# The second MLP layer's column halves run two row blocks apart, and its outputs leave one per chunk

## The chip, the cores and the metric

The kernel runs on one core of a Trainium2 chip. The metric is the device time of one execution in microseconds; a kernel's time is the median of its runs. TensorE (PE in the profile) multiplies, VectorE (DVE) and ScalarE (ACT) work on tiles in SBUF and PSUM, SyncE (SP) issues the loads and the last stores, GpSimd (POOL) issues the other transfers. Each engine runs its instructions in an order that is fixed when the program is built, and waits on semaphores where an operand is not there yet.

## The reference, cut to what matters

One layer on 512 tokens of 2048 features, in float32:

```python
hn = rms_norm(x, norm_mix)
x = x + neighbourhood_attention(hn, w_qkv, q_gain, k_gain, rel_bias, w_o)
h = rms_norm(x, norm_mlp)
a = relu(h @ w1)          # w1: 2048 x 8192
x = x + (a * a) @ w2      # w2: 8192 x 2048
```

The change touches the last line alone: a product of 512 x 8192 by 8192 x 2048, added to the residual.

## The kernel before

The program has four stages: the projections and the attention, the output projection (whose residual sum goes to `y_sum` in DRAM), the first layer of the MLP (from 778.1 us of the span), and the second (from 1419.6 us to the end).

**Units and chunks.** Both MLP layers are cut into `Pair` units. A unit multiplies all 512 tokens by a weight block of 2048 rows and 1024 columns: four blocks of 512 rows (b = 0 to 3), each seen as a 2 x 2 matrix of quarters, multiplied by seven products instead of eight. `Pair.chunks()` lists the 28 pairs (m, b): first m = 1, 5, 6, 4 for each block in turn (FIRST, chunks 0 to 15), then m = 2, 3, 7 for each block (SECOND, chunks 16 to 27). A chunk is one 128 x 1024 weight tile of 512 KB and twelve 128 x 512 matmuls on it (L248). The first layer has eight units, h0 to h7; the second has eight, yc_p, where c (0 to 3) is the four blocks of rows and p (0, 1) the half of the 2048 output columns; they run y0_0, y0_1, y1_0 and so on to y3_1.

**What a chunk needs.** SP loads the weight tile (L193) some six chunks ahead. For m = 5, 6, 4 and 7 DVE adds the tile before it (L217). ACT makes the high part `wh` (L233), DVE the rest `wl` (L235), both about three chunks ahead of the matmuls. DVE does its instructions in program order, so a tile that isn't there holds all that stands behind it. Raw tiles rotate through ten buffers (`raw`), high and low parts through three (`hl`): a load is issued only when the `wl` that read the buffer's old tile is done.

**Left operands.** h units leave squared activations; `left_window` turns them by 32 transposes per unit in eight windows and writes seven left operands for each block of rows to `z_t` in DRAM (POOL: L710, L711, L721). A y unit needs 28 of them, each 256 KB as read, for its four blocks. `pass_on` loads them (L759, on SP) one after each chunk of the unit before and splits them 1.5 chunks later (a step, `STEP`, is a quarter of a chunk's work; ACT L554, DVE L556). The two units of one c use the same operands, so h7, y0_1, y1_1 and y2_1 carry 28 such loads, and y0_0, y1_0, y2_0, y3_0 and y3_1 none.

**Outputs.** The products end in PSUM banks named x, y, z and w in the trace. At the end of a unit `evict` makes eight tiles of 256 KB: two `c` behind m = 2 of the last block, two `u` behind m = 3, and `t`, `p`, `t`, `p` behind m = 7. `take_out` sends each at once as an accumulating DMA on POOL's queue (L748) to `y_sum`, 48 in all; the units of c = 3 add `y_sum`, loaded ahead by `prefetch`, and store to the output on SP's queue (L746).

**What sets the order.** `run` emits chunk by chunk; `u.after` is called behind each chunk's matmuls; `later(lag, fn)` puts a step off by so many positions. From that the framework's scheduler makes each engine's order: it keeps roughly to the order of emission, but lets an instruction go ahead that it takes to be ready. So loads and adds (L217) may stand up to nine chunks ahead of their matmuls on SP and DVE, further than the six and three chunks that `run` gives them.

Of the kernel before, what the change touches and what calls it, by code (L numbers as in the profile page):

```python
# [14 lines left out]
ALU = mybir.AluOpType  # L15
AX = mybir.AxisListType

P = 128
T = 512
D = 2048  # L20
# [5 lines left out]
NCH = HID // D  # L26
# [6 lines left out]
NB = KT // 4  # L33
# [8 lines left out]
STEP, WAIT, PAIR = 1, 5, 3  # L42


class Unit:
# [7 lines left out]
    def __init__(self, name, src, act, done, kind):  # L53
        self.name, self.src, self.act, self.done, self.kind = name, src, act, done, kind
        self.n = KT // 4 if kind == "narrow" else KT
        self.raw, self.parts, self.ps = {}, {}, None
        self.load, self.before, self.after, self.lag = None, None, None, 0


class Pair:  # L60
# [16 lines left out]
    QUARTER = {1: (0, 0), 5: (0, 1), 6: (1, 1), 4: (1, 0), 2: (1, 0), 3: (1, 1), 7: (0, 1)}  # L77
    CHAIN = {5: 1, 6: 5, 4: 6, 7: 3}

    def __init__(self, name, w, row, col, comb, take):  # L80
        self.name, self.w, self.row, self.col, self.comb, self.take = name, w, row, col, comb, take
        self.raw, self.parts, self.banks, self.after = {}, {}, {}, None
        self.t, self.u, self.p4, self.p5 = {}, {}, {}, {}

    def chunks(self):
        return [(self, (m, b)) for stage in (self.FIRST, self.SECOND) for b in range(NB) for m in stage]

    def quarter(self, m, b):
        r, c = self.QUARTER[m]
        r, c = self.row + (4 * b + 2 * r) * P, self.col + c * T  # L90
        return self.w[r // (2 * P), c // T]


# [1 line left out]
def natten_mlp_kernel(ctx, tc, x_t, gains, w_qk, w_v, bias, w_o, w1, w2, out_t):  # L95
    nc = tc.nc
# [8 lines left out]
    def wtile(name, dt=F32):  # L105
        return tiles.tile([P, T], dt, tag="w", name=name)

    def bank(name):
        return psum.tile([P, T], F32, tag="b", name=name)
# [8 lines left out]
    def kept(ins):  # L118
        return tc.keep_in_program_order(ins) if pos[0] < pinned else ins

    def pair(name):
        return wtile(f"{name}h", F32R), wtile(f"{name}l", F32R)
# [49 lines left out]
    def later(lag, fn):  # L172
        side.append((pos[0] + lag, fn))

    def start(steps):

        wait = next(steps, None)
        if wait is not None:
            later(wait, lambda: start(steps))

    def run_side(until):
        while True:
            due = sorted((s for s in side if s[0] <= until), key=lambda s: s[0])
            if not due:
                return
            for s in due:
                side.remove(s)
                s[1]()
# [20 lines left out]
    def split_raw(u, i, first):  # L209
# [22 lines left out]
        else:  # L232
            kept(nc.scalar.activation(h, s, AF.Copy))  # L233
            yield 2 * STEP
            kept(nc.vector.tensor_tensor(out=l, in0=s, in1=h.bitcast(F32), op=ALU.subtract))  # L235

    def multiply_pair(u, i):
        m, b = i
        x = u.BANK[m]
        if x not in u.banks:  # L240
            u.banks[x] = [bank(f"{x}_{u.name}_{j}") for j in range(2)]
        wh, wl = u.parts.pop(i)
        ah, al = u.comb[b][m]
        for k in range(2):
            for j in range(2):
                c = slice(k * HALF + j * P, k * HALF + (j + 1) * P)
                for n, (a, w) in enumerate(((ah, wh), (ah, wl), (al, wh))):
                    nc.tensor.matmul(out=u.banks[x][j], lhsT=a[:, c], rhs=w[:, k],  # L248
                                     start=(m in u.FIRST and b + k + n == 0), stop=(b == NB - 1 and k == 1 and n == 2),
                                     skip_group_check=True)  # L250
                pos[0] += 1
                if 2 * k + j < 3:
                    run_side(pos[0])
        if b == NB - 1:
            start(evict(u, m))
        if u.after is not None:
            u.after(m, b)
        run_side(pos[0])
# [153 lines left out]
    class Head:  # L412
        def __init__(self, h):
            self.h = h
            self.p = {}
# [105 lines left out]
    for g in range(NG):  # L521
        u = Unit(f"v{g}", lambda i, g=g: w_v[i // 2, g], xa, v_done(g), "tokens")
# [24 lines left out]
    xc = [{} for _ in range(NB)]  # L547
    sq_a = wtile("sq_a")

    def parts_of(dst, m, src, name):  # L550

        h, l = pair(name)
        view = lambda z: z.rearrange("p (k n) -> p k n", k=2)
        nc.scalar.activation(view(h), src, AF.Copy)  # L554
        yield STEP
        nc.vector.tensor_tensor(out=view(l), in0=src, in1=view(h).bitcast(F32), op=ALU.subtract)  # L556
        dst[m] = (h, l)
        yield STEP
# [28 lines left out]
    y_sum = {(c, n): dram.tile([P, T], F32, name=f"y_{c}_{n}", tag=f"y_{c}_{n}") for c in range(QB) for n in range(NG)}  # L587
# [16 lines left out]
    def window():  # L604
        if windows:
            windows.pop(0)()
# [49 lines left out]
    for g in range(NG):  # L656
        u = Unit(f"o{g}", lambda i, g=g: w_o[i // 2, g], oa, o_done(g), "wide")
# [6 lines left out]
    FP = HID // (2 * T)  # L664

    z_t = [dram.tile([P, 7, 2, HALF], F32, name=f"z_{i}", tag=f"z_{i}") for i in range(2 * FP)]
# [8 lines left out]
    def take_hidden(p):  # L675
        zs = {}

        def take(c, half, src, add, minus=False):
            if add is None:
                t = wtile(f"z_{p}_{c}_{half}")  # L680
            else:
                t = join(src, add, minus)
                src = t
            nc.scalar.activation(t, src, AF.Relu, scale=r_a[:, c:c + 1])
            zs[c, half] = t
            if len(zs) == 8:
                for n in range(8):
                    windows.append(left_window(p, n // 4, n // 2 % 2, n % 2, zs))
        return take
# [35 lines left out]
    def take_out(p, last):  # L725
        ys = {}

        def prefetch():
            for c in range(QB):
                for half in range(2):  # L730
                    ys[c, half] = wtile(f"ys_{p}_{c}_{half}")
                    nc.sync.dma_start(out=ys[c, half], in_=y_sum[c, 2 * p + half])

        def take(c, half, src, add, minus=False):
            rows, cols = slice(c * P, (c + 1) * P), slice((2 * p + half) * T, (2 * p + half + 1) * T)
            if add is not None:
                if last:
                    nc.vector.tensor_tensor(out=add, in0=add, in1=ys[c, half], op=ALU.add)
                t = join(src, add, minus)
            elif last:  # L740
                t = join(src, ys[c, half], False)
            else:
                t = wtile(f"c_{p}_{c}_{half}")
                nc.scalar.activation(t, src, AF.Copy)
            if last:
                nc.sync.dma_start(out=out_t[rows, cols], in_=t)  # L746
            else:
                nc.gpsimd.dma_start(out=y_sum[c, 2 * p + half], in_=t, accum_op=ALU.add)  # L748
        return take, prefetch

    def pass_on(dst, block):


        order = (2, 4, 1, 5, 6, 3, 7)
        loaded = {}

        def load(m, b):
            t = loaded[m, b] = wtile(f"zr{m}_z{block}_{b}")
            nc.sync.dma_start(out=t.rearrange("p (k n) -> p k n", k=2), in_=z_t[4 * block + b][:, order.index(m)])  # L759

        def split_left(m, b):
            yield from parts_of(dst[b], m, loaded.pop((m, b)).rearrange("p (k n) -> p k n", k=2), f"a{m}_z{block}_{b}")

        def after(m, b):
            load(m, b)
            later(6 * STEP, lambda: start(split_left(m, b)))
        return after

    pairs, comb = [], xc
    for p in range(FP):  # L770
        u = Pair(f"h{p}", w1, 0, 2 * p * T, comb, take_hidden(p))
        pairs.append(u)
    zc = [[{} for _ in range(NB)] for _ in range(NCH)]
    for c in range(NCH):
        for p in range(2):
            take, prefetch = take_out(p, c == NCH - 1)
            u = Pair(f"y{c}_{p}", w2, c * D, 2 * p * T, zc[c], take)
            u.prefetch = prefetch if c == NCH - 1 else None
            pairs.append(u)
    for n, u in enumerate(pairs):  # L780
        hand = None
        if n >= FP - 1 and (n - FP + 1) % 2 == 0 and n < len(pairs) - 1:
            block = (n - FP + 1) // 2
            hand = pass_on(zc[block], block)

        def after(m, b, n=n, u=u, hand=hand):
            if m in u.SECOND:
                if n == 0 and m == 2 and b == 0:
                    start(norm_a())
                window()  # L790
            if m == 4 and b == NB - 1 and n >= FP and u.prefetch is not None:
                u.prefetch()
            if hand is not None:
                hand(m, b)
        u.after = after
        chunks += u.chunks()

# [53 lines left out]
```

## Time and profile before

| | us |
|---|---|
| median of three runs | 2081.96 (2080.67 to 2084.63) |
| the profiled execution | 2081.29 |
| its span, first to last instruction | 2079.5 |
| second MLP layer, in that span | 1419.6 to 2073.5 |

Engines, busy share of the span: PE 98%, weight loads 81%, DVE 74%, ACT 50%, POOL 6%. The mean granted clock of TensorE is 0.995 of its full level.

With PE busy nearly all the time there are two things to look for in a stretch: how long it takes beside another with the same matmuls, and whether PE is idle in it or busy for longer at a lower clock. A table by stretches shows both: its length, PE's busy time, the granted clock and the busy share of the DMA engines. A timeline of one engine shows how long it sat idle ahead of an instruction and what released it; a list by one source line gives the time from a DMA's issue to its landing.

### The profile page before, as it was taken

How to read it: one execution, taken by the hardware profiler on the slowest of the kernel's cores; microseconds unless marked ns; L12 is line 12 of the kernel's file. 1: busy time of each engine (PE TensorE's matmuls, PEld its weight loads, DVE VectorE, ACT ScalarE, POOL GpSimd, SP SyncE). 2: the span in 40 equal slices, each digit the busy share in tenths (PEclk: the TensorE clock that was granted, in tenths of full speed). 3: DMA queues.
4: the chain of work that ended last, by engine and by line, in shares of the span. 5: the costliest groups of instructions: out<-in, count | busy, mean ns of one | idle time of the engine just before them, and what ended most of it. 6: DMA issues, size and time to landing. Idle time of an engine off the chain costs nothing. (4 is left out here: it accounts for less than half of the span.)

```text
span 2079.5 us, 25226 instructions
## 1 busy us (share of the span) xinstructions
PE 2044.1 (98%) x9330; PEld 1684.3 (81%) x9330; DVE 1546.5 (74%) x1884; ACT 1045.5 (50%) x1412; POOL 116.7 (6%) x166
## 2 busy tenths in 40 slices
PE   9999999999999999999999999999989999999998
PEld 7888888888888888888888888887877877778787
DVE  6674674774774469778878878798879778779786
ACT  6663563653663445544545545565445445346333
POOL 0000000000000000010110110100201011010000
PEclk9999999999999999999999999999999999999999
DMA  7222222222233346565866757778689598688874
GB/s 289 101 92 83 100 92 92 96 90 96 99 101 127 112 137 211 193 217 199 274 202 226 269 180 255 270 255 304 226 295 286 187 272 279 204 261 278 256 243 147
DMA packets 127900, 400.15 MB, mean 192 GB/s; under 512 B 15008, under 2 KB 15008, under 8 KB 127776
## 3 DMA queue, kind: packets, MB, share of 16 engines
q1 hardware_dynamic: 110736, 352.37, 50.3%
q0 software_dynamic: 16896, 46.15, 7.8%
q8 instruction: 73, 1.20, 0.2%
q14 instruction: 51, 0.42, 0.1%
q10 hardware_dynamic: 144, 0.02, 0.0%
HBM read 348.14 MB, written 50.33 MB: 192 GB/s over the span
## 5 line engine op out<-in xcount | busy, mean ns | idle before, releaser
L233 ACT ACTIVATE wh_h<-w_h 128x1024 fp32r<-128x1024 f32 x224 | 237.6, 1060 | 275.0 <-PE y_h L248 83.7
L233 ACT ACTIVATE wh_y<-w_y 128x1024 fp32r<-128x1024 f32 x224 | 236.5, 1059 | 234.2 <-PE y_y L248 69.0
L235 DVE TENSOR_TENSOR wl_h<-w_h,wh_h 128x1024 fp32r<-128x1024 f32 x224 | 272.8, 1221 | 77.4 <-ACT wh_h L233 76.7
L235 DVE TENSOR_TENSOR wl_y<-w_y,wh_y 128x1024 fp32r<-128x1024 f32 x224 | 271.0, 1219 | 24.5 <-ACT wh_y L233 24.0
L217 DVE TENSOR_TENSOR w_y<-w_y,w_y 128x1024 f32<-128x1024 f32 x128 | 156.1, 1220 | 70.9 <-DMA w_y<-in_w 68.1
L217 DVE TENSOR_TENSOR w_h<-w_h,w_h 128x1024 f32<-128x1024 f32 x128 | 155.1, 1219 | 42.9 <-DMA w_h<-in_w 42.8
L235 DVE TENSOR_TENSOR wl_o<-w_o,wh_o 128x1024 fp32r<-128x1024 f32 x32 | 39.1, 1223 | 58.7 <-ACT wh_o L233 58.6
L233 ACT ACTIVATE wh_o<-w_o 128x1024 fp32r<-128x1024 f32 x32 | 33.9, 1059 | 80.0 <-PE mm_o L302 66.2
L233 ACT ACTIVATE wh_q<-w_q 128x1024 fp32r<-128x1024 f32 x32 | 34.0, 1062 | 77.8 <-PE mm_q L302 30.2
L235 DVE TENSOR_TENSOR wl_q<-w_q,wh_q 128x1024 fp32r<-128x1024 f32 x32 | 39.2, 1225 | 43.6 <-ACT wh_q L233 42.3
L235 DVE TENSOR_TENSOR wl_k<-w_k,wh_k 128x1024 fp32r<-128x1024 f32 x32 | 39.1, 1222 | 37.9 <-ACT wh_k L233 37.9
L233 ACT ACTIVATE wh_k<-w_k 128x1024 fp32r<-128x1024 f32 x32 | 34.0, 1062 | 50.8 <-PE mm_q L302 31.1
L233 ACT ACTIVATE wh_v<-w_v 128x1024 fp32r<-128x1024 f32 x31 | 32.8, 1058 | 47.4 <-PE mm_v L302 23.4
L235 DVE TENSOR_TENSOR wl_v<-w_v,wh_v 128x1024 fp32r<-128x1024 f32 x31 | 37.9, 1223 | 23.0 <-ACT wh_v L233 22.6
L600 POOL DMA_DIRECT2D y<-x1t_0s x4 | 2.3, 583 | 770.1 <-ACT x1t_0s L599 770.1
L711 POOL DMA_DIRECT2D z<-zt x32 | 17.7, 553 | 453.0 <-ACT zt L706 452.9
L554 ACT ACTIVATE a_z_0h<-zr_z 128x512 fp32r<-128x512 f32 x28 | 17.6, 627 | 50.4 <-DMA zr_z<-z 48.5
L509 ACT ACTIVATE t<-t,st 128x256 f32<-128x256 f32 x64 | 32.0, 501 | 10.6 <-DVE st L505 10.6
L706 ACT ACTIVATE zt<-zt 128x512 f32<-128x512 f32 x64 | 37.1, 580 | 0.0
L248 PE MATMUL y_y<-wl_y,a_z_1h 128*128 128x512 f32 x64 | 26.6, 416 | 8.4 <-DVE wl_y L235 8.4
L248 PE MATMUL z_y<-wl_y,a_z_0h 128*128 128x512 f32 x64 | 26.7, 418 | 6.8 <-DVE wl_y L235 6.8
L554 ACT ACTIVATE a_z_3h<-zr_z 128x512 fp32r<-128x512 f32 x28 | 17.5, 626 | 29.6 <-DMA zr_z<-z 29.6
(1435 smaller groups left out, 6304.2 us busy)
## 6 DMA issues: line engine op xcount, KB each, us to landing
w_h<-in_w SPq DMA_DIRECT2D x224, 512.0 KB, 4.3
w_y<-in_w SPq DMA_DIRECT2D x224, 512.0 KB, 4.6
zr_z<-z SPq DMA_DIRECT2D x112, 256.0 KB, 5.3
w_q<-in_w_qk SPq DMA_DIRECT2D x32, 512.0 KB, 3.5
w_k<-in_w_qk SPq DMA_DIRECT2D x32, 512.0 KB, 3.5
w_o<-in_w_o SPq DMA_DIRECT2D x32, 512.0 KB, 3.5
w_v<-in_w_v SPq DMA_DIRECT2D x31, 512.0 KB, 3.5
z<-zt POOLq DMA_DIRECT2D x32, 256.0 KB, 3.9
```

Source lines behind the costliest of these rows:

```text
L217: nc.vector.tensor_tensor(out=s, in0=s, in1=u.raw[u.CHAIN[m], b], op=ALU.add)
L233: kept(nc.scalar.activation(h, s, AF.Copy))
L235: kept(nc.vector.tensor_tensor(out=l, in0=s, in1=h.bitcast(F32), op=ALU.subtract))
L248: nc.tensor.matmul(out=u.banks[x][j], lhsT=a[:, c], rhs=w[:, k], start=(m in u.FIRST and b + k + n == 0), stop=(b == NB - 1 and k == 1 and ...
L509: nc.scalar.activation(halves[i], halves[i], AF.Exp, bias=st[:, i:i + 1], accum_out=st[:, 2 + i:3 + i])
L554: nc.scalar.activation(view(h), src, AF.Copy)
L600: nc.gpsimd.dma_start(out=dst, in_=t)
L706: nc.scalar.activation(t[:, i], ps, AF.Square)
L711: nc.gpsimd.dma_start(out=dst[:, 2], in_=t[:, 0, :HALF])
```

## The change

- The second layer has nine units, y0 to y8, in place of eight. The column halves alternate (p = 1, 0, 1, ...), and each unit starts two blocks of rows after the one before: blocks 0-1, 0-3, 2-5, 4-7, 6-9, 8-11, 10-13, 12-15, 14-15. y0 and y8 have two blocks (14 chunks), the others four (28). All 224 chunks and their matmuls remain; each column half is done in one more unit, or none more: p = 1 in y0, y2, y4, y6, y8, p = 0 in y1, y3, y5, y7. So there are 56 accumulating outputs in place of 48. The last two units store directly, as the last two did before.
- Left operands: blocks c and c + 1 leave with unit n, and after each of their 14 chunks the operand of block c + 4 or c + 5 is loaded. So y1 to y6 each load 14, behind their first eight FIRST and first six SECOND chunks. h7 loads blocks 0 and 1 as before, blocks 2 and 3 with a lag of 48 steps, twelve chunks.
- Outputs are put in a list, `outs`, and `send`, called behind each chunk, issues one, with a wait for the newest matmul emitted so far.
- h7's eight left windows come behind y0's six SECOND chunks: a second window behind each m = 7.

```diff
-    def __init__(self, name, w, row, col, comb, take):
+    def __init__(self, name, w, blocks, col, comb, take):
     def chunks(self):
-        return [(self, (m, b)) for stage in (self.FIRST, self.SECOND) for b in range(NB) for m in stage]
+        return [(self, (m, b)) for stage in (self.FIRST, self.SECOND) for b in self.blocks for m in stage]
...
+                    newest[0] = nc.tensor.matmul(out=u.banks[x][j], lhsT=a[:, c], rhs=w[:, k],
+                                                 start=(m in u.FIRST and b == u.blocks[0] and k + n == 0),
+                                                 stop=(b == u.blocks[-1] and k == 1 and n == 2),
+                                                 skip_group_check=True)
...
-                nc.gpsimd.dma_start(out=y_sum[c, 2 * p + half], in_=t, accum_op=ALU.add)
+                outs.append((y_sum[c, 2 * p + half], t))
...
+    outs = []
+    def send():
+        if outs:
+            dst, t = outs.pop(0)
+            ins = nc.gpsimd.dma_start(out=dst, in_=t, accum_op=ALU.add)
+            tc.add_manual_dep(ins.ins, newest[0].ins.name,
+                              mybir.DependencyInfo(mybir.DependencyClass.Sync, mybir.DependencyReason.DATA),
+                              reason="pace")
...
         def after(m, b):
-            load(m, b)
-            later(6 * STEP, lambda: start(split_left(m, b)))
+            if b in heirs:
+                wait = 48 * STEP if heirs[b] == b >= 2 else 0
+                later(wait, lambda: load(m, heirs[b]))
+                later(wait + 6 * STEP, lambda: start(split_left(m, heirs[b])))
...
+    for n in range(2 * NCH + 1):
+        p, c = 1 - n % 2, 2 * n - 2
+        rows = range(max(c, 0), min(c + NB, NCH * NB))
+        take, prefetch = take_out(p, n >= 2 * NCH - 1)
+        u = Pair(f"y{n}", w2, rows, 2 * p * T, zc, take)
...
+        c = 2 * (n - FP) - 2
+        if n == FP - 1:
+            hand = pass_on({b: b for b in u.blocks})
+        elif n > FP and c + NB < NCH * NB:
+            hand = pass_on({c: c + NB, c + 1: c + NB + 1})
...
                 window()
+                if n == FP and m == 7:
+                    window()
...
             if hand is not None:
                 hand(m, b)
+            send()
```

On POOL, at the seam between the first layer's left operands and the outputs of the first y unit, before: the last writes of left operands (`z`), then the eight outputs of y0_0, each waiting only for the engine that made its tile and for its queue slot (`DMASW`).

```order
L711 DMA z_140<-zt_1_1_12366 128x256 [waits DMASW5_49,Activation_49]
L710 DMA z_140<-zt_1_1_12366 128x2x256 [waits DMASW6_49,Activation_49]
L721 DMA z_140<-zt_1_1s 128x4x256 [waits DMASW7_49,DVE_49]
L748 DMA y_0_108<-c_0_0_12438 128x512 [waits DMASW0_49,Activation_49]
L748 DMA y_0_112<-c_1_0_12450 128x512 [waits DMASW1_49,Activation_49]
L748 DMA y_1_109<-u_y_0_0_12146 128x512 [waits DMASW2_49,DVE_49]
L748 DMA y_1_113<-u_y_0_1_12157 128x512 [waits DMASW3_49,DVE_49]
L748 DMA y_0_116<-t_y_0_0_12102 128x512 [waits DMASW4_49,DVE_49]
```

The same place with the change:

```order
L760 DMA y_2_110<-c_0_0_12125 128x512 [waits DMASW1_49,PE_49,Activation_49]
L724 DMA z_139<-zt_0_1s 128x4x256 [waits DMASW2_49,DVE_49]
L760 DMA y_2_114<-c_1_0_12146 128x512 [waits DMASW3_49,PE_49,Activation_49]
L714 DMA z_140<-zt_1_0_12132 128x256 [waits DMASW4_49,Activation_49]
L713 DMA z_140<-zt_1_0_12132 128x2x256 [waits DMASW5_49,Activation_49]
L760 DMA y_3_111<-u_y_0_11960 128x512 [waits DMASW6_49,DVE_49,PE_49]
L714 DMA z_140<-zt_1_1_12209 128x256 [waits DMASW7_49,Activation_49]
L713 DMA z_140<-zt_1_1_12209 128x2x256 [waits DMASW0_49,Activation_49]
L724 DMA z_140<-zt_1_0s 128x4x256 [waits DMASW1_49,DVE_49]
```

The outputs now wait for PE too, and they stand between the last writes of left operands, which so queue behind matmuls.

On DVE, at the start of the unit behind the first one with loads, before (y1_0, behind y0_1): the last `u` of the old unit, then at once the low part of the new unit's second chunk.

```order
L672 TENSOR_TENSOR u_y_1_1_12883<-z_y_1_1_12520,u_y_1_1_12883 128x512
L235 TENSOR_TENSOR wl_y_0_5_13186<-w_y_0_5_13073,wh_y_0_5_13185 128x1024
L556 TENSOR_TENSOR a_z_3l<-zr_z_3_13147,a_z_3h 128x512
L672 TENSOR_TENSOR t_y_1_0_12814<-y_y_1_0_12542,t_y_1_0_12814 128x512
L670 TENSOR_TENSOR p_y_1_0_12842<-p_y_1_0_12842,y_y_1_0_12542 128x512
L672 TENSOR_TENSOR t_y_1_1_12826<-y_y_1_1_12543,t_y_1_1_12826 128x512
```

With the change, at the start of y2 (and of y3 to y6 alike), behind y1:

```order
L675 TENSOR_TENSOR u_y_1_12589<-z_y_1_12256,u_y_1_12589 128x512
L217 TENSOR_TENSOR w_y_5_12948<-w_y_5_12948,w_y_1_12920 128x1024
L235 TENSOR_TENSOR wl_y_5_12855<-w_y_5_12763,wh_y_5_12854 128x1024
L675 TENSOR_TENSOR t_y_0_12534<-y_y_0_12279,t_y_0_12534 128x512
L673 TENSOR_TENSOR p_y_0_12556<-p_y_0_12556,y_y_0_12279 128x512
L675 TENSOR_TENSOR t_y_1_12544<-y_y_1_12280,t_y_1_12544 128x512
```

An add on a weight tile needed eight chunks later (the tenth chunk of y2) now stands ahead of the low part of the second chunk; the splits of left operands are gone from this place.

## Rows read from the trace of the kernel before

**Rows 1.** Stretches: start:end, length, PE busy (x), PEclk, DMA share, GB/s.

```profile
858.30:938.30 80.00, 80.00 (x369) 1.00 0.64 214
1419.60:1502.20 82.60, 81.13 (x370) 1.00 0.72 245
1502.20:1587.90 85.70, 78.88 (x338) 0.96 0.92 295
1587.90:1667.70 79.80, 77.34 (x337) 1.00 0.71 212
1667.70:1753.50 85.80, 80.20 (x337) 0.96 0.89 278
1753.50:1834.10 80.60, 77.73 (x338) 1.00 0.72 214
1834.10:1918.60 84.50, 79.57 (x338) 0.98 0.91 281
1918.60:1997.20 78.60, 77.06 (x338) 1.00 0.80 251
1997.20:2073.50 76.30, 76.30 (x337) 1.00 0.54 189
```

**Rows 2.** Waits of PE, 1415 to 2080: total us, times, longest us.

```profile
PE y_y L248 <- DVE wl_y L235: 10.4, 10, 2.1
PE z_y L248 <- DVE wl_y L235: 6.8, 2, 4.2
```

**Rows 3.** Timeline of DVE at the start of y2_1 (1834.1).

```profile
1832.06 1.28 DVE L672 TENSOR_TENSOR u_y<-z_y,u_y 128x512 f32<-128x512 f32 x2
1837.38 1.23 DVE L217 TENSOR_TENSOR w_y<-w_y,w_y 128x1024 f32<-128x1024 f32 x1 [4.04 <-DMA w_y<-in_w]
1838.52 1.22 DVE L235 TENSOR_TENSOR wl_y<-w_y,wh_y 128x1024 fp32r<-128x1024 f32 x1
```

**Rows 4.** Timeline of PE, the same place.

```profile
1839.79 0.50 PE L248 MATMUL z_y<-wl_y,a_z_0h 128*128 128x512 f32 x1 [2.62 <-DVE wl_y L235]
```

**Rows 5.** Timeline of POOL, the same place.

```profile
1829.04 0.86 POOL L748 DMA_DIRECT2D y<-c  x1 [68.47 <-ACT c L744]
1830.66 0.86 POOL L748 DMA_DIRECT2D y<-c  x1 [0.77 <-ACT c L744]
1833.04 1.75 POOL L748 DMA_DIRECT2D y<-u_y  x2 [1.51 <-DVE u_y L672]
```

**Rows 6.** The one weight load (L193) that the add waited for there.

```profile
L193 SPq DMA_DIRECT2D w_y<-in_w x1: 328/328/328, 1831.0 to 1831.0; - x1
DMA to landing us min/median/max: 6.2/6.2/6.2
```

**Rows 7.** The page's DMA issues: count, KB each, us to landing (no outputs beside them).

```profile
w_o<-in_w_o SPq DMA_DIRECT2D x32, 512.0 KB, 3.5
```

**Rows 8.** Timeline of ACT in y2_1, chunks 5 and 6.

```profile
1853.40 0.63 ACT L554 ACTIVATE a_z_0h<-zr_z 128x512 fp32r<-128x512 f32 x1 [5.34 <-DMA zr_z<-z]
```

**Rows 9.** Two weight loads (L193) two apart in SP's order, no outputs in flight.

```profile
L193 SPq DMA_DIRECT2D w_y<-in_w x1: 328/328/328, 1426.1 to 1426.1; - x1
DMA to landing us min/median/max: 5.1/5.1/5.1
...
L193 SPq DMA_DIRECT2D w_y<-in_w x1: 382/382/382, 1427.0 to 1427.0; - x1
DMA to landing us min/median/max: 6.7/6.7/6.7
```

**Rows 10.** Two weight loads (L193) in a row, among the outputs of y0_0.

```profile
L193 SPq DMA_DIRECT2D w_y<-in_w x1: 411/411/411, 1503.7 to 1503.7; - x1
DMA to landing us min/median/max: 14.2/14.2/14.2
...
L193 SPq DMA_DIRECT2D w_y<-in_w x1: 395/395/395, 1504.2 to 1504.2; - x1
DMA to landing us min/median/max: 16.3/16.3/16.3
```

**Rows 11.** All 48 accumulating outputs (L748).

```profile
DMA to landing us min/median/max: 4.7/8.9/16.2
```

More of the change, by code (lines that the diff above doesn't have):

```diff
@@ L78 @@
     CHAIN = {5: 1, 6: 5, 4: 6, 7: 3}
-    def __init__(self, name, w, row, col, comb, take):
-        self.name, self.w, self.row, self.col, self.comb, self.take = name, w, row, col, comb, take
+    def __init__(self, name, w, blocks, col, comb, take):
+        self.name, self.w, self.blocks, self.col, self.comb, self.take = name, w, blocks, col, comb, take
         self.raw, self.parts, self.banks, self.after = {}, {}, {}, None
@@ L85, in chunks @@
     def chunks(self):
-        return [(self, (m, b)) for stage in (self.FIRST, self.SECOND) for b in range(NB) for m in stage]
+        return [(self, (m, b)) for stage in (self.FIRST, self.SECOND) for b in self.blocks for m in stage]
     def quarter(self, m, b):
         r, c = self.QUARTER[m]
-        r, c = self.row + (4 * b + 2 * r) * P, self.col + c * T
+        r, c = (4 * b + 2 * r) * P, self.col + c * T
         return self.w[r // (2 * P), c // T]
@@ L235, in split_raw @@
             kept(nc.vector.tensor_tensor(out=l, in0=s, in1=h.bitcast(F32), op=ALU.subtract))
+    newest = [None]
     def multiply_pair(u, i):
@@ L247, in multiply_pair @@
                 for n, (a, w) in enumerate(((ah, wh), (ah, wl), (al, wh))):
-                    nc.tensor.matmul(out=u.banks[x][j], lhsT=a[:, c], rhs=w[:, k],
-                                     start=(m in u.FIRST and b + k + n == 0), stop=(b == NB - 1 and k == 1 and n == 2),
-                                     skip_group_check=True)
+                    newest[0] = nc.tensor.matmul(out=u.banks[x][j], lhsT=a[:, c], rhs=w[:, k],
+                                                 start=(m in u.FIRST and b == u.blocks[0] and k + n == 0),
+                                                 stop=(b == u.blocks[-1] and k == 1 and n == 2),
+                                                 skip_group_check=True)
                 pos[0] += 1
@@ L253, in multiply_pair @@
                     run_side(pos[0])
-        if b == NB - 1:
+        if b == u.blocks[-1]:
             start(evict(u, m))
@@ L747, in take, with pass_on @@
             else:
-                nc.gpsimd.dma_start(out=y_sum[c, 2 * p + half], in_=t, accum_op=ALU.add)
+                outs.append((y_sum[c, 2 * p + half], t))
         return take, prefetch
-    def pass_on(dst, block):
+    outs = []
[6 more added lines that the diff above has]
+                              reason="pace")
+    def pass_on(heirs):
         order = (2, 4, 1, 5, 6, 3, 7)
@@ L757, in load @@
         def load(m, b):
-            t = loaded[m, b] = wtile(f"zr{m}_z{block}_{b}")
-            nc.sync.dma_start(out=t.rearrange("p (k n) -> p k n", k=2), in_=z_t[4 * block + b][:, order.index(m)])
+            t = loaded[m, b] = wtile(f"zr{m}_z_{b}")
+            nc.sync.dma_start(out=t.rearrange("p (k n) -> p k n", k=2), in_=z_t[b][:, order.index(m)])
         def split_left(m, b):
-            yield from parts_of(dst[b], m, loaded.pop((m, b)).rearrange("p (k n) -> p k n", k=2), f"a{m}_z{block}_{b}")
+            yield from parts_of(zc[b], m, loaded.pop((m, b)).rearrange("p (k n) -> p k n", k=2), f"a{m}_z_{b}")
@@ L764, in after @@
         def after(m, b):
-            load(m, b)
-            later(6 * STEP, lambda: start(split_left(m, b)))
-        return after
-    pairs, comb = [], xc
-    for p in range(FP):
-        u = Pair(f"h{p}", w1, 0, 2 * p * T, comb, take_hidden(p))
-        pairs.append(u)
[L773 to L779, printed above, removed]
@@ L780, in natten_mlp_kernel @@
-    for n, u in enumerate(pairs):
[L781 to L784, printed above, removed]
+            if b in heirs:
+                wait = 48 * STEP if heirs[b] == b >= 2 else 0
+                later(wait, lambda: load(m, heirs[b]))
+                later(wait + 6 * STEP, lambda: start(split_left(m, heirs[b])))
+        return after
+    pairs = [Pair(f"h{p}", w1, range(NB), 2 * p * T, xc, take_hidden(p)) for p in range(FP)]
@@ new lines, in natten_mlp_kernel @@
+    zc = [{} for _ in range(NCH * NB)]
+    for n in range(2 * NCH + 1):
[3 more added lines that the diff above has]
+        u = Pair(f"y{n}", w2, rows, 2 * p * T, zc, take)
+        u.prefetch = prefetch if n >= 2 * NCH - 1 else None
+        pairs.append(u)
+    for n, u in enumerate(pairs):
+        c = 2 * (n - FP) - 2
[3 more added lines that the diff above has]
+            hand = pass_on({c: c + NB, c + 1: c + NB + 1})
+        else:
+            hand = None
@@ L790, in after @@
                 window()
-            if m == 4 and b == NB - 1 and n >= FP and u.prefetch is not None:
+                if n == FP and m == 7:
+                    window()
+            if m == 4 and b == u.blocks[-1] and n >= FP and u.prefetch is not None:
                 u.prefetch()
```

## The prediction

> **What bounds the kernel now.** I read first the table of stretches, cut at the units of the second layer, to see how much one unit takes longer than another with the same matmuls [rows 1]. The last unit, y3_1, has 28 chunks and takes 76.3 us with PE busy throughout: 28 chunks at 2.725 us. That is the floor of a unit. A unit of the first layer has the same chunks and 32 transposes and takes 80.0, so the transposes cost 3.7. Against these two, y0_0 (28 chunks and h7's transposes) loses 82.6 - 80.0 = 2.6, and the others, in order, 9.4, 3.5, 9.5, 4.3, 8.2, 2.3 and 0. The sum, 39.8 us, is nearly all that a change of this stage can win, since matmuls and transposes stay the same in number: it would end at 2081.3 - 39.8 = 2041.5.
>
> The losses follow a pattern. The three units that carry left-operand loads lose 8.2 to 9.5, those without 2.3 to 4.3. The former show a DMA share of 0.89 to 0.92 against 0.71 to 0.80, and a granted clock of 0.96 to 0.98 where the others have 1.00 [rows 1]. With the same count of matmuls, PE is busy for 78.9, 80.2 and 79.6 us in them and for 77.1 to 77.7 in the others: some 2 us of the loss is the lower clock, which the table shows only where PE also stood idle, and the rest is idle time. The waits of PE say for what: nearly all for the low part `wl` of a weight tile, which DVE makes [rows 2].
>
> Then I followed one such wait back. At the start of y2_1 PE stands for 2.62 us ahead of its second chunk [rows 4], for a `wl` that DVE began at 1838.52. DVE had been idle for 4.04 us, not for that tile but for an add (L217) on another one that stands ahead of it in its order [rows 3]. That add's tile is needed eight chunks later; its load was issued only at 1831.0, when its buffer came free, and landed after 6.2 us [rows 6]. The same load with nothing beside it takes 3.5 [rows 7]. Just ahead of it two `c` outputs were issued, at 1829.04 and 1830.66, and two `u` at 1833.04 [rows 5]. So landing less PE's wait is 6.2 - 2.6 = 3.6: that is the allowance, and a quiet load just fits. The longest such wait of PE, 4.2 us [rows 2], is the same place in y1_1. A second wait comes four chunks later, where ACT stands for 5.34 us for a left operand in the same traffic [rows 8], and PE then for up to 2 us.
>
> **What the traffic can carry.** Two weight loads with another between them, no outputs in flight: one issued at 1426.1 lands after 5.1, one at 1427.0 after 6.7 [rows 9], so they end 2.5 apart and one tile of 512 KB takes 1.25 us of the DMA engines. Among the outputs of y0_0, two loads in a row, issued at 1503.7 and 1504.2, land after 14.2 and 16.3 [rows 10], 2.6 apart: an output of 256 KB between each two takes some 1.3. A left operand, half a tile, I put at half of 1.25, 0.65. A chunk of 2.72 us with one tile, one output and one left operand then needs 1.25 + 1.3 + 0.65 = 3.2, half a microsecond too much; without the left operand 2.55, which fits.
>
> **The change part by part.** *Outputs one per chunk.* They leave over eight chunks (22 us) instead of in bursts of two, two and four. Each now waits for a matmul of its chunk, and on POOL only outputs are queued behind it in y2 to y8; in y0's end and y1's start, the last writes of left operands are too. At the start of a unit the first `c` still goes ahead of the critical weight load, the second about a chunk later, behind it. So the load meets one output where it met two to four. Its landing lies between 3.5 (the output is through) and 6.2 (as now); with one output's 1.3 in front I take 4.9, a wait of 4.9 - 3.6 = 1.3 in place of 2.6 to 4.2.
>
> *Where DVE's add stands.* The order shows that y2 to y6 begin like y1_1 and y2_1 did: the add stands ahead of the second chunk's `wl`. So five units have the exposed place, where two had it. At 1.3 each that is 6.5, about the 2.6 + 4.2 = 6.8 of now; this part gains nothing by itself, and is a loss if pacing doesn't help.
>
> *Left operands.* The loads stay 112 in number, and 14 fall into each of y1 to y6, beside the first eight FIRST and six SECOND chunks, in place of 28 in three units. In the first eight chunks with outputs they make the 3.2 us above. Loads begin some three chunks into the unit, so five chunks lose 0.5 each: a backlog of 2.5 us at its worst, about half of the 5.34 that ACT waited [rows 8]. PE then waits for 0.7 (0 to 2). In the second group there are no outputs, and nothing waits. With shorter waits I take 0.8 us for the clock, not 2.
> A unit of y2 to y6 so loses 1.3 + 0.7 + 0.8 = 2.8, bounded by 0.2 (all hidden, as in y3_1) and by 8 (as the loaded units now).
>
> *The ends.* y0 has the same eight windows as y0_0, in 14 chunks instead of 28; it lost 2.6, I take 3 (2 to 6). y1 starts with y0's outputs, h7's last writes of left operands and loads of its own together. Its like is y0_1, 9.4; spread outputs and half the loads bring it part of the way to 2.8, and I take 6 (3 to 10). y7 has no loads but starts with outputs, like y3_0 with 2.3; I take 1.5. y8, like y3_1, 0.2. h7 stays as it is: half of its loads now fall into y0, but the other half are at its start, where they are today.
>
> The eight further outputs are eight issues of some 0.86 us on POOL [rows 5], which has little else in that stage, and some 8 x 1.3 = 10 us of transfers within the traffic counted above; twelve further DVE instructions at some 0.64 us, like the two `u` in 1.28 [rows 3], lie beside PE's 2.72 per chunk. Both I cost at nothing as long as DVE has no wait for a tile; where it has, the adds of the eighth unit more, y0, wait along.
>
> Sum: 3 + 6 + 5 x 2.8 + 1.5 + 0.2 = 24.7 against 39.8, a gain of 15. On the profiled execution 2081.3 - 15.1 = 2066.2; the median of the runs is 0.7 above that execution, so **2067**.
>
> **A rule on what an output costs.** The accumulating outputs land after 4.7 to 16.2 us, 8.9 in the median [rows 11], and in traffic one takes 1.3 us of the engines [rows 9, 10], as much as a weight load twice its size. The Trainium skill, "DMA: Bandwidth & Descriptors", section "Anatomy of one DMA — SWDGE (gpsimd) path", gives a GpSimd DMA about 2.0 us of fixed cost and its bytes at 436 GB/s beside; that is, as an estimate from the page, 0.6 us of moving for 256 KB. By it, a chunk would need 1.25 + 0.6 + 0.65 = 2.5 us and no backlog would arise; the trace speaks against it, with 2.6 us for a tile and an output. What a chunk that fits would make of the time is the second rival, below.
>
> **The rivals.** *Slower: the loaded units stay as dear, and there are more of them.* The place is the start of each of y1 to y6: paced outputs are in flight for eight chunks instead of three, all of them together with left-operand loads, and the exposed add stands in five units. For it: 3.2 us of transfers in 2.72. Against it: half the loads, and no burst. If each of the six loses 7.5, the sum is 45 + 4.7 = 49.7, ten more than now: 2091; at 8.5, 2097. It decides from a loss of (39.8 - 4.7) / 6 = 5.85 per loaded unit on.
> *Near the floor.* If a chunk's transfers fit in it, the load at the start lands before it is needed, and the loaded units lose 0.8: 6 x 0.8 + 4 = 9, a gain of 31, 2051. For it: y3_1, at 0 [rows 1]; against it, the 2.6 us of [rows 10].
> *The burst isn't the cause.* The two `c` alone, issued ahead of the load [rows 5], may make it late, and the wait for a matmul moves the second too little. Then five units keep waits of 2.6 to 4.2 and their clock, some 5.8 each with y1: no change, 2082. That is also what comes if the wait for the newest matmul is already met when POOL comes to it.
>
> **How the numbers follow.** About 0.2%, 4 us, is what a measurement of this kernel can tell from no change. Forecast (a gain of 5 to 25, 2057 to 2077): 0.50. Near the floor: 0.08. No change (within 4 to 5 us): 0.16. Slower: 0.26. Faster is 0.58, same 0.15, slower 0.27. To leave out no more than 2 in 10 the range goes from 2050, the floor rival's, to 2091, the slower rival's first value; beyond each lie some 0.05 and 0.13. The forecast's own range is 2057 to 2077.
>
> **What would show it.** Right: at the start of y2 to y6, DVE's idle time ahead of the add is 1.5 to 3 us, not 4 to 5.4, and the load there lands after about 5; units y2 to y6 last 78 to 80 us with a clock of 0.98 or more; no accumulating output lands after more than some 10 us beyond y1; the outputs lie 2.7 us apart. y0 lasts about 38.2 + 3.7 + 3 = 45 and y1 82. Wrong: units of 82 or more with a clock of 0.96, ACT's waits for left operands of 5 us as before, or outputs that start two at a time.

## The result: slower, and where the time went

| | median us | runs |
|---|---|---|
| before | 2083.15 (2080.67 to 2084.63) | 4 |
| with the change | 2101.07 (2098.29 to 2105.89) | 4 |
| ratio | 1.0090, 95% interval 1.0067 to 1.0112 | |

The change costs 18 us. I had forecast a gain of 15 and a range that ended at 2091, so neither the sign nor the range held. The profiled execution took 2098.29 us with a span of 2096.5, 17.0 longer than that of before.

The stretches of the second layer answer to [rows 1]. They are, in order, y0 to y8; the columns are start:end, length, PE busy (x), granted clock, DMA share, GB/s.

```profile
1425.90:1468.90 43.00, 42.41 (x202) 1.00 0.73 262
1468.90:1557.70 88.80, 80.55 (x340) 0.98 0.86 279
1557.70:1640.10 82.40, 78.81 (x337) 1.00 0.78 245
1640.10:1723.30 83.20, 79.55 (x338) 0.96 0.80 249
1723.30:1807.30 84.00, 78.80 (x337) 1.00 0.80 242
1807.30:1890.20 82.90, 79.55 (x337) 0.96 0.79 247
1890.20:1973.10 82.90, 78.30 (x338) 1.00 0.80 251
1973.10:2052.40 79.30, 77.30 (x337) 1.00 0.78 240
2052.40:2090.60 38.20, 38.20 (x169) 1.00 0.51 188
```

Against the floors of the prediction (76.3 for 28 chunks, half of it and 3.7 for y0), the losses are 1.2, 12.5, 6.1, 6.9, 7.7, 6.6, 6.6, 3.0 and 0: 50.6, in place of the 39.8 of before and the 24.7 of the forecast. Only y1 is dearer than the units with loads were, but six units now lose 6 us or more where three did. PE stood idle for 20.4 us of the 33.9 that y2 to y6 lost (length less busy time in the table); the rest is longer busy time.

That is 10.8 of the 17.0. Another 4.4 came in the first layer's first unit, 84.6 us against 80.2, and 1.5 ahead of that, where the two programs have the same instructions in the same order. A second profile of the changed kernel, below, has that unit at 81.6, so 3.0 of the 4.4 was chance of that execution. That execution had larger losses in the second layer instead: these stretches are its y1 and y4.

```profile
1465.20:1555.80 90.60, 81.02 (x338) 0.98 0.84 273
...
1721.40:1807.50 86.10, 80.45 (x338) 0.96 0.78 237
```

The losses of its y0 to y7 are 1.8, 14.3, 6.0, 7.0, 9.8, 5.2, 9.9 and 5.3, together 59.3, or 19.5 more than before, for an execution of 2102.6. The loss of a unit varies by up to 3.3 us between the two executions; that each of y1 to y6 has one of 5 us or more doesn't.

**The start of a unit.** This is DVE, then PE, at the start of y3 (1640.1), which answers to [rows 3] and [rows 4].

```profile
1638.51 1.28 DVE L675 TENSOR_TENSOR u_y<-z_y,u_y 128x512 f32<-128x512 f32 x2
1644.21 1.23 DVE L217 TENSOR_TENSOR w_y<-w_y,w_y 128x1024 f32<-128x1024 f32 x1 [4.42 <-DMA w_y<-in_w]
1645.35 1.22 DVE L235 TENSOR_TENSOR wl_y<-w_y,wh_y 128x1024 fp32r<-128x1024 f32 x1
...
1642.85 0.39 PE L250 MATMUL z_y<-wh_y,a_z_4h 128*128 128x512 f32 x1
1646.62 0.80 PE L250 MATMUL z_y<-wl_y,a_z_4h 128*128 128x512 f32 x1 [3.38 <-DVE wl_y L235]
1647.21 0.63 PE L250 MATMUL z_y<-wh_y,a_z_4l 128*128 128x512 f32 x1
```

It reads as [rows 3] did: two `u`, then an add that waits, then the low part that PE waits for. The next fences show what was issued around the load, POOL's outputs and SP's loads, and its landing.

```profile
1634.99 0.84 POOL L760 DMA_DIRECT2D y<-c  x1 [60.03 <-PE x_y L250]
1637.71 0.85 POOL L760 DMA_DIRECT2D y<-c  x1 [1.88 <-DVE wl_y L235]
```

```profile
1637.48 0.33 SPq L193 DMA_DIRECT2D w_y<-in_w  x1
1637.86 0.90 SPq L773 DMA_DIRECT2D zr_z<-z  x2
```

```profile
L193 SPq DMA_DIRECT2D w_y<-in_w x1: 328/328/328, 1637.5 to 1637.5; - x1
DMA to landing us min/median/max: 6.6/6.6/6.6
```

The outputs are 2.7 us apart, as the edit says. But the second `c` goes 0.2 us behind the critical load, and two left-operand loads 0.4 us behind it. The load landed after 6.6 us, no sooner than the 6.2 of [rows 6]. In y4, where the second `c` and the first left operand each went 0.4 us behind it, it landed after 4.9, as I had taken it for every unit:

```profile
L193 SPq DMA_DIRECT2D w_y<-in_w x1: 328/328/328, 1720.6 to 1720.6; - x1
DMA to landing us min/median/max: 4.9/4.9/4.9
```

### The profile page after: what moved, and what is told of

It reads as the page before. It is cut to its first block, busy times and chain, and to the rows that moved or that the text cites. A ratio compares the mean times of both kernels' runs of the same rounds, so it can differ in the third digit from the quotient of the medians.

```text
span 2096.5 us, 25260 instructions
## 1 busy us (share of the span) xinstructions
PE 2054.2 (98%) x9330; PEld 1688.0 (81%) x9330; DVE 1555.4 (74%) x1896; ACT 1045.3 (50%) x1416; POOL 122.6 (6%) x174
## 5 line engine op out<-in xcount | busy, mean ns | idle before, releaser
L235 DVE TENSOR_TENSOR wl_y<-w_y,wh_y 128x1024 fp32r<-128x1024 f32 x224 | 270.8, 1218 | 14.3 <-ACT wh_y L233 14.1
L233 ACT ACTIVATE wh_o<-w_o 128x1024 fp32r<-128x1024 f32 x32 | 33.9, 1059 | 80.0 <-PE mm_o L305 66.2
L235 DVE TENSOR_TENSOR wl_k<-w_k,wh_k 128x1024 fp32r<-128x1024 f32 x32 | 39.1, 1222 | 37.9 <-ACT wh_k L233 37.9
L235 DVE TENSOR_TENSOR wl_v<-w_v,wh_v 128x1024 fp32r<-128x1024 f32 x31 | 37.9, 1224 | 24.0 <-ACT wh_v L233 23.7
L714 POOL DMA_DIRECT2D z<-zt x32 | 18.1, 565 | 441.9 <-ACT zt L709 441.8
L760 POOL DMA_DIRECT2D y<-c x14 | 12.0, 855 | 372.9 <-PE x_y L250 359.7
L713 POOL DMA_DIRECT2D z<-zt x32 | 22.7, 709 | 70.6 <-ACT zt L709 70.4
L250 PE MATMUL z_h<-wh_h,a_x1h 128*128 128x512 f32 x64 | 26.4, 412 | 0.0
L250 PE MATMUL y_h<-wh_h,a_x1h 128*128 128x512 f32 x64 | 26.2, 409 | 0.0
```

The source lines that it names most:

```text
L250: newest[0] = nc.tensor.matmul(out=u.banks[x][j], lhsT=a[:, c], rhs=w[:, k], start=(m in u.FIRST and b == u.blocks[0] and k + n == 0), sto ...
L713: nc.gpsimd.dma_start(out=dst[:, 0:2], in_=t[:, 1].rearrange("p (m n) -> p m n", m=2))
L714: nc.gpsimd.dma_start(out=dst[:, 2], in_=t[:, 0, :HALF])
L760: ins = nc.gpsimd.dma_start(out=dst, in_=t, accum_op=ALU.add)
```

## The experiments

Four theories stood. **A**: DVE's order is the cause; an add that stands ahead of an urgent instruction waits for a late load, and the stagger gives five units that place. **B**: sending one output per chunk costs by itself. **C**: the left-operand loads, or the outputs, are the heavier part of the traffic. **D**: the DMA engines are short of time in these chunks, whatever the order.

### Each half of the change alone

The changed kernel with its outputs sent as they are made:

```diff
-                outs.append((y_sum[c, 2 * p + half], t))
+                nc.gpsimd.dma_start(out=y_sum[c, 2 * p + half], in_=t, accum_op=ALU.add)
```

> The changed kernel with its outputs sent as soon as they are made, as in the kernel before; the two-block stagger stays. Theory A (the add that stands ahead of the second chunk's low part waits for a load that is late in the traffic, and the stagger gives five units this place where two had it): the two c outputs again go ahead of the load, it lands after 6 to 8 us, and y2 to y6 lose 7 to 10 each: 2103 to 2115. Rival B (sending one per chunk is what costs, since outputs are in flight for eight chunks beside left-operand loads): without it the time falls back to 2080 to 2090.

2109.33 us (ratio to before 1.0121, 1.0098 to 1.0145). Theory A's range; y2 to y6 lost 7.5 to 10.5. Pacing isn't the culprit: without it the staggered kernel is no faster, and by the two ratios some 6 us slower, though their intervals overlap.

The kernel before with the list, `send` and its wait, as in the change's diff, and nothing else of it:

> The kernel before with one edit of the change alone: outputs one per chunk, each with the wait for the newest matmul. Theory A: the exposed place exists in y1_1 and y2_1 only; there the load meets one output in place of two, and the wait shrinks by 1 to 2 us each: 2076 to 2083. Rival B: outputs in flight for eight chunks beside 28 left-operand loads cost more than the bursts: 2088 to 2095.

2075.79 (ratio 0.9972, 0.9957 to 0.9988), at the lower end of theory A's range. Faster by 0.3%; rival B falls in this kernel too. Pacing helps by itself, and the stagger without it costs 25 us (1.0121), so the loss is the stagger's. Why is the question of the other runs. My reason for pacing's gain was only partly right: in y1_1 of this kernel the critical load still landed after 6.3 us, with the second `c` 0.7 us behind it.

### What the traffic consists of

Outputs left out (y0 to y6 make them, but nothing is added to the sum in memory):

```diff
-                outs.append((y_sum[c, 2 * p + half], t))
+                pass
```

> The changed kernel with the outputs of y0 to y6 left out (made, but not added to the sum in memory), so that no accumulating transfer runs in this stage. Theory A: the load at the start of y2 to y6 meets only two left operands, lands after 4 to 5 us and PE waits 1 us or less there; y2 to y6 lose 1 to 3: 2070 to 2082. Rival C' (left-operand loads are the heavier part): y2 to y6 lose 4 to 6: 2085 to 2093.

2062.91 (two executions; ratio 0.9908, 0.9875 to 0.9940), 7 us below theory A's range. DVE's order at the units' starts is the same as in the changed kernel, so this prices the outputs in that order: some 38 us hang on them. The stretches of y2 and y3:

```profile
1543.90:1622.40 78.50, 77.44 (x337) 1.00 0.69 234
1622.40:1700.20 77.80, 76.82 (x338) 1.00 0.71 238
```

y2 to y6 lose 1.2 to 3.0, as theory A had it, and y1 4.3 in place of 12.5. The critical load of y3, with the same two left-operand loads 0.4 us behind it, landed nearly as fast as the quiet load of [rows 7]:

```profile
L193 SPq DMA_DIRECT2D w_y<-in_w x1: 328/328/328, 1619.7 to 1619.7; - x1
DMA to landing us min/median/max: 3.7/3.7/3.7
```

Left-operand loads and their splits left out (from y1 on the old operands are multiplied again):

```diff
             if b in heirs:
+                if heirs[b] != b:
+                    zc[heirs[b]][m] = zc[b][m]
+                    return
```

> The changed kernel with the left-operand loads and their splits left out from y1 on (the old operands are multiplied again). Theory A with outputs as the main traffic: the load meets one output or two, and y2 to y6 lose 2 to 4: 2075 to 2085. Rival C' (the left operands are the heavier part): they lose 1 or less: 2065 to 2073.

2087.09 (ratio 1.0029, 1.0013 to 1.0046), 2 us above the range for theory A. Even without a single left operand, y2 to y6 lose 3.5 to 7.7. It isn't a clean price: with the splits gone the scheduler let the adds go further ahead still (in the mean 6.8 low parts ahead of their own tile's, counted in DVE's order, against 6.4), and DVE waited for their loads for longer. This is DVE's wait in the changed kernel, then in this one (total us, times, longest).

```profile
DVE w_y L217 <- DMA w_y<-in_w: 87.9, 53, 4.4
```

```profile
DVE w_y L217 <- DMA w_y<-in_w: 149.7, 72, 6.2
```

Less traffic, and longer waits for it: that points to the order and away from the DMA engines' time. The critical load of y3, now with outputs and no left operand, landed as late as in the changed kernel:

```profile
L193 SPq DMA_DIRECT2D w_y<-in_w x1: 327/327/327, 1629.7 to 1629.7; - x1
DMA to landing us min/median/max: 6.6/6.6/6.6
```

So at this place the outputs made the load late, and the left-operand loads did not: theory C is settled for the outputs.

Left-operand loads eight chunks later:

```diff
-                wait = 48 * STEP if heirs[b] == b >= 2 else 0
+                wait = 48 * STEP if heirs[b] == b >= 2 else 0 if heirs[b] == b else 32 * STEP
```

> The changed kernel with the left-operand loads of y1 to y6 eight chunks (32 steps) later, so that they miss the outputs. Theory A in its form that left-operand loads share the engines with the critical load at the unit's start (it landed after 6.6 us in y3 and y5 with two of them issued right behind it): the load meets one output only, lands after 4 to 5, and y2 to y6 lose 3 to 4 in place of 6.3 to 7.9: 2083 to 2090. Rival C (outputs alone make it late): 2097 to 2102, the same as now.

2098.16 (ratio 1.0069, 1.0051 to 1.0087): in rival C's range, and by the intervals not to be told from the changed kernel. The edit was not a clean test. Eight chunks behind the second group is the end of the unit and the next one's start, so that group took the first one's place beside the outputs; and the order changed with it, so that at the start of y3 no add stands ahead of the second chunk's `wl`. But its waits are instructive. First the changed kernel's, then this one's:

```profile
PE z_y L250 <- DVE wl_y L235: 15.0, 10, 3.4
```

```profile
PE x_y L250 <- DVE wl_y L235: 11.6, 8, 5.7
PE y_y L250 <- DVE wl_y L235: 7.4, 11, 1.6
PE y_y L250 <- ACT wh_y L233: 6.0, 4, 1.8
...
PE z_y L250 <- DVE wl_y L235: 1.9, 2, 1.1
```

The bank `z` is the second chunk's. The wait that I had followed is nearly gone, and the time isn't: other chunks wait in its place.

### The order on DVE

All adds of the second layer pinned to the order in which the program emits them, two chunks ahead of their matmuls:

```diff
-                nc.vector.tensor_tensor(out=s, in0=s, in1=u.raw[u.CHAIN[m], b], op=ALU.add)
+                ins = nc.vector.tensor_tensor(out=s, in0=s, in1=u.raw[u.CHAIN[m], b], op=ALU.add)
+                if u.name[0] == "y":
+                    tc.keep_in_program_order(ins)
```

> The changed kernel with the adds on weight tiles (L217) of the second layer kept in the order in which the program emits them, so that each stands two chunks ahead of its matmuls on DVE and not eight or nine. Theory A: a late load then holds nothing that is needed sooner, the wait at each unit's second chunk goes, and y2 to y6 lose 1 to 3 in place of 6.3 to 7.9: 2070 to 2080. Rival D (the DMA engines are short of time in these chunks, whatever DVE's order): the waits move to the tile itself and the time stays within 5 us of 2101.

2061.17 (ratio 0.9888, 0.9867 to 0.9910): 40 us below the changed kernel, 9 below theory A's range, by an edit that takes away no work and no transfer. Theory D, as stated, falls. The stretches of y2, y3, y4 and y6:

```profile
1551.30:1628.60 77.30, 76.90 (x337) 1.00 0.88 266
1628.60:1707.70 79.10, 77.28 (x337) 1.00 0.84 258
1707.70:1785.10 77.40, 76.89 (x337) 1.00 0.86 263
...
1862.20:1942.60 80.40, 78.44 (x338) 0.98 0.84 255
```

y2 to y6 lose 0.8 to 4.1, at a higher DMA share than the 0.78 to 0.80 of the changed kernel.

The same edit on the kernel before, and on the paced kernel before:

> The kernel before with one edit: the adds (L217) of the second layer kept in program order. Theory A (order on DVE is the cause, in both kernels): the waits at the second chunk of y1_1 and y2_1 and those at chunks 5 and 6 that come from adds go, 15 to 20 us in all: 2060 to 2068. Rival E (the order cures only what the stagger made): 2075 to 2083, about as before.

2058.35 (ratio 0.9892, 0.9872 to 0.9912), 2 us under theory A's range. The order was the larger part of the loss in the kernel before, too.

> The kernel before with the adds in program order and outputs one per chunk, without the two-block stagger. If pacing still matters with the order mended, it is 2 to 5 us under the one with the adds alone: 2056 to 2064. If late loads hold nothing any more, both are equal within 2 us. Against the changed kernel with the adds kept (2061) it tells what the stagger is worth by itself: theory A, nothing or a loss from its first two units: 2055 to 2061; rival F, the halved loads help once the order is mended: this one is 3 to 8 us slower than 2061.

2060.14 (ratio 0.9894, 0.9878 to 0.9909). The three ratios with the adds kept, 0.9888, 0.9892 and 0.9894, can't be told apart: once the order is mended, neither pacing nor the stagger changes the time by more than these runs can show, some 4 us. Both halves of the change act through the waits that the order makes.

Was it that one add? Only the add of the tenth chunk pinned:

```diff
+                if u.name[0] == "y" and m == 5 and u.blocks[2:3] == range(b, b + 1):
+                    tc.keep_in_program_order(ins)
```

> The changed kernel with one add of each unit y1 to y7 kept in program order: that of the tenth chunk, which stood ahead of the second chunk's low part and now stands behind the sixth's. Theory A (this one add carries the loss at the units' starts): the waits of 1.6 to 3.4 us at the second chunk of y2 to y6 go with the low clock behind them, 12 to 18 us in all: 2083 to 2089. Rival G (any add with a late load will do; the next one in the order takes its place): 2095 to 2101.

2103.08 (ratio 1.0099, 1.0079 to 1.0119): no gain, as rival G said (2 us above its range). The waits on bank `z` fall from 15.0 us to 2.8, and PE waits in other places, for ACT among them:

```profile
PE y_y L252 <- ACT wh_y L235: 7.4, 6, 2.0
...
PE z_y L252 <- DVE wl_y L237: 2.8, 2, 1.9
```

With that add out of the way, the scheduler set the splits of left operands sooner, and ACT comes to left operands that haven't landed. It did so in the changed kernel, too (6.61 us of idle time ahead of its first split in y3), but there DVE's wait held PE at the same time. This is ACT in y3 with the one add pinned:

```profile
1639.22 0.63 ACT L559 ACTIVATE a_z_8h<-zr_z 128x512 fp32r<-128x512 f32 x1 [6.05 <-DMA zr_z<-z]
...
1646.27 0.63 ACT L559 ACTIVATE a_z_8h<-zr_z 128x512 fp32r<-128x512 f32 x1 [3.06 <-DMA zr_z<-z]
```

So theory A as I stated it, one add at one place, falls. What holds is its wider form: another instruction that stands early in an in-order queue and reads a late transfer takes over; here these were the splits on ACT and other adds on DVE.

### Both orders mended

With the adds kept, the kernel before still lost 7.1 in y0_1, to such a split on ACT (9.88 us of idle time ahead of it). So the splits go later as well:

```diff
-            later(6 * STEP, lambda: start(split_left(m, b)))
+            later(16 * STEP, lambda: start(split_left(m, b)))
```

> The kernel before with the adds in program order, and with the splits of left operands 16 steps behind their loads in place of 6, so that ACT does not come to a left operand that is still on its way among the outputs of y0_0. The wait of 4.5 us of PE in y0_1 that stood with the adds alone should go, with 2 us of low clock: 2050 to 2054. If the splits are needed as early as they were, or other waits come forward, no gain: 2057 to 2062.

2044.85 (2044.25 to 2045.39; ratio 0.9816, 0.9801 to 0.9831), 5 us under the range that I expected, and within 4 of the floor that the prediction worked out for a stage without waits (2041.5). It beats both kernels. The stretches of y0_1, y1_0 and y1_1:

```profile
1501.00:1577.10 76.10, 76.10 (x337) 1.00 0.99 333
1577.10:1654.10 77.00, 76.71 (x337) 1.00 0.77 224
1654.10:1730.30 76.20, 76.20 (x338) 1.00 0.95 311
```

y0_1 is at the floor with a DMA share of 0.99, and outputs still leave in bursts. A weight load in this stretch:

```profile
L193 SPq DMA_DIRECT2D w_y<-in_w x1: 328/328/328, 1503.8 to 1503.8; - x1
DMA to landing us min/median/max: 17.5/17.5/17.5
```

It landed after 17.5 us, later than the 16.3 of [rows 10], and PE lost nothing.

The same two edits on the changed kernel:

> The changed kernel with the adds in program order and the left-operand splits 16 steps behind their loads: the stagger and the pacing upon the two edits that brought the kernel before to 2044.85. Theory A (with DVE's and ACT's orders mended, late landings hold nothing, and the stagger keeps only its dear first two units, 7.5 and 9.2 us with the adds alone): y2 to y6 lose 1 or less, 2050 to 2056, above 2044.85. Rival F (halving the left-operand loads is worth something of its own): 2040 to 2045.

2049.45 (ratio 0.9829, 0.9798 to 0.9860), half a microsecond under theory A's range, and rival F falls; the intervals of the two ratios overlap, so the stagger is worth nothing that shows in the time. In the profile y1 to y4 are:

```profile
1465.80:1547.20 81.40, 77.75 (x340) 1.00 0.91 305
1547.20:1623.30 76.10, 76.10 (x337) 1.00 0.84 269
1623.30:1699.50 76.20, 76.20 (x338) 1.00 0.85 269
1699.50:1775.60 76.10, 76.10 (x337) 1.00 0.84 268
```

From y2 on it loses nothing, with the outputs and left-operand loads in the same eight chunks. A weight load among the outputs at the start of y2 landed far later than the 6.6 of the changed kernel, and nothing waited for it:

```profile
L193 SPq DMA_DIRECT2D w_y<-in_w x1: 333/333/333, 1544.6 to 1544.6; - x1
DMA to landing us min/median/max: 9.6/9.6/9.6
```

What is left is 2.2 in y0 and 5.1 in y1. In y1 PE stood once for 3.36 us, for a `wl` that stood behind an add on DVE, and the add's load landed only after 11.9 us among the outputs of y0. Whether order could cure that too, or the transfers bound it there, no run tried.

### The changed kernel once more

> The changed kernel once more, unchanged, for the spread of its times and for the stages ahead of the change: in its first profile the first MLP unit took 84.6 us against 80.2 before, with the same order of instructions. Theory: chance of that execution; the unit takes 80 to 81 and the median is 2095 to 2101. Rival: it belongs to the kernel: 84 to 85 again.

2104.31 (ratio 1.0095, 1.0064 to 1.0127), above the range that I gave; its executions run from 2095.71 to 2107.38. The first unit of the first layer was at 81.6, nearer to theory than to rival. Its stretches stand in the section on the result.

## Why the prediction was wrong, step by step

- **What bounds the kernel** was right: the floor of 2041.5 was all but reached (2044.85) with no edit but two of order, and the chain from PE through `wl` to an add ahead of it in DVE's order was the true one at that place.
- **The step that failed is the price of a loaded unit.** I had 2.8 for y2 to y6, 14 in all; they lost 33.9 in one profile (6.1 to 7.7 each) and 37.9 in the other (5.2 to 9.9). Of the 33.9, 11.6 are the waits at the second chunk, put at 6.5, another 8.8 are other waits of PE, put at 3.5 for left operands, and 13.5 are longer busy time, where I had put 4 for the clock. Where all of that busy time comes from stays open.
- **Where DVE's add stands** was right in the count (five units with the place in place of two) and wrong in the price. I took 1.3 us for the wait; it was 1.3 to 3.4 in one profile and 1.3 to 4.9 in the other, and in the first the clock is at 0.96 in the units with the longer waits, y3 and y5. The landing of 4.9 came in y4; in y3 and y5 it was 6.6. The allowance was too large as well: landing less PE's wait is 3.2 in all five units, not 3.6.
- **Outputs one per chunk** failed there: "the load meets one output where it met two to four". It met the second `c`, too, issued 0.2 to 0.5 us behind it in y3 to y6. Over the two profiles and the run without left operands, the load landed after 6.3 to 8.1 us in the eight cases with the second `c` less than 0.3 us behind it, after 4.9 to 6.6 with it 0.3 to 0.5 behind, and after 4.5 to 5.2 where the two were about 1 us apart. By these cases an output issued just behind the load makes it late, too; no run varied that alone.
- **Left operands** had an error of reading. I let their loads begin some three chunks into the unit, where the splits begin; SP issues them 0.4 us behind the critical load (1637.86 against 1637.48), as the trace of before had:

```profile
1831.03 0.33 SPq L193 DMA_DIRECT2D w_y<-in_w  x1
1831.45 0.95 SPq L759 DMA_DIRECT2D zr_z<-z  x2
```

  This put my backlog in the wrong chunks, but it isn't what made the critical load late: that load landed after 3.7 us with them and without outputs.
- **The first and last units.** y1, put at 6, lost 12.5 and 14.3: its loss without outputs, 4.3, shows that y0's outputs made two thirds of the 12.5. y0 (3) and y8 (0.2) were near, at 1.2 to 1.8 and 0; y7 (1.5) lost 3.0 and 5.3.
- **The slower rival** had the price. I gave it 7.5 to 8.5 for each of six units, 2091 to 2097; they lost 7.7 on average in the first profile (12.5 + 33.9 over six) and 8.7 in the second. It had a chance of 0.26, and I cut the range at its lower value; its upper one still lay under 2101.
- **Its mechanism was wrong.** I argued it from 3.2 us of transfers in a chunk of 2.72. With the same transfers in the same chunks and both orders mended, y2 to y7 lose nothing at a share of 0.81 to 0.85. The transfers made the landings late; the orders made late landings cost. By the price that the Trainium skill gives for a GpSimd DMA ("DMA: Bandwidth & Descriptors", "Anatomy of one DMA — SWDGE (gpsimd) path") no backlog arises, which was the rival near the floor; that price is 2.6 us for 256 KB as an estimate from the page, and in the changed kernel's traffic the outputs landed after 4.0 to 10.8 us. No run here has an output alone.
- **Pacing** was right in sign: a gain of 0.3% alone, and by the ratios some 6 us under the stagger, where the two intervals overlap.

## What to carry to other kernels

Ahead of changing transfers, look at what stands in front of the waiting instruction on its own engine. If an in-order queue holds an early instruction on a tile that isn't needed for many chunks, late transfers cost there. Here moving transfers about moved the waits to others and gained 0.3% at best; pinning the adds took away no work and gave 22 us in the kernel before, 38 with later splits, where the rearrangement was forecast to give 15 and cost 18. A change that multiplies an exposed place must be priced at the measured wait of today, not at the wait that another edit of the same change is hoped to leave.

## What the runs showed of the hardware

A stretch with a DMA share of 0.99 and loads that land after 17.5 us ran PE without a wait: the share of busy time of the DMA engines didn't tell whether they bounded it. A weight load with an output 2.5 us ahead of it and one 0.2 us behind it, both from POOL, landed after 6.6 us (with the left operands left out); with two left-operand loads 0.4 and 0.9 us behind it and no outputs it landed after 3.7.

In the stretches shown the clock is under 1.00 only in units in which PE also stood idle. After the wait of 3.38 us in y3 a matmul took 0.63 us, where one took 0.39 ahead of it; after 1.65 us in y4 they stayed at 0.39 and the clock at 1.00. So the longer wait cost more than its own length. But the clock isn't all of the longer busy time: y4 was busy for 78.80 us at a clock of 1.00, where the same unit of the mended kernel took 76.10.
